# First MLP product of a two-layer transformer trunk by Strassen's 2x2 block form, on one Trainium2 core

## The chip, the cores and the metric

The kernel runs on one core of a Trainium2 chip. The time is the device time of one execution in microseconds (us). Five engines work side by side, each through its own queue of instructions in order: TensorE (PE in the profile, its weight loads PEld), VectorE (DVE), ScalarE (ACT), GpSimd (POOL) and SyncE (SP, which here only issues transfers). Fewer microseconds are better.

## The reference

Two layers work on 512 latent tokens and 256 context tokens of 1024 features. Each has adaLN-modulated RMSNorm, one input projection, a gMLP mixer beside grouped-query attention, an output projection, and then the part that the change touches:

```python
def sqrelu_mlp(h, w1, w2):
    return jnp.square(jax.nn.relu(h @ w1)) @ w2
...
    for l in range(DEPTH):                                   # DEPTH = 2
        last = l == DEPTH - 1
        m_lat = modulation(c, w_mod[l], b_mod[l])
        m_ctx = modulation(c_ctx, w_mod[l], b_mod[l])
        ...
        x_lat = x_lat + ga2 * sqrelu_mlp(modulate(rmsnorm(x_lat, norm2_g[l]), sh2, sc2),
                                         w_ff1[l], w_ff2[l])
        if not last:
            ...
            x_ctx = x_ctx + cga2 * sqrelu_mlp(modulate(rmsnorm(x_ctx, norm2_g[l]), csh2, csc2),
                                              w_ff1[l], w_ff2[l])
    return x_lat
```

`w_ff1[l]` is 1024 x 4096, `w_ff2[l]` 4096 x 1024, all float32. The MLP of layer 0 runs over 768 tokens, that of layer 1 over the 512 latent ones.

## The kernel before

**Products in split form.** Each float32 operand is held as a high part `hi` in TensorE's reduced float32 format and the remainder `lo`. `split` (L207, L208) makes them: ACT casts the raw tile to `hi`, DVE subtracts `hi` from the raw tile for `lo`. A product is three matmuls, hi x hi, hi x lo and lo x hi (`mm`, L203). Activations lie features first: an MLP feature tile is 128 features (partitions) by all tokens, and a product over 1024 input features is 8 x 3 matmuls per token part. Layer 0 has two token parts of 384 columns, layer 1 one of 512.

**Weight stream.** Weights come as blocks of 128x1024 in the order of use (`block_order`). `pump` issues a block's transfer on SP into one of two raw buffers, then splits it into one of four ring slots (`hi` and `lo` tiles). It goes on as long as slots are free; `release` gives a slot back once the last matmul that reads it is written.

**MLP.** Eight chunks of four feature tiles. `ff1` computes one tile with w_ff1 in PSUM tile `pa`, and `relu2` squares its ReLU and splits the square: ACT ReLU (L954) and Square (L959), DVE product (L960) and difference (L961), into a `B` home, of which eight hold two chunks of tiles. `proj4` then takes the four blocks of w_ff2 of the chunk (called first to fourth second-product block below), eight output tiles of 4 x 3 matmuls each per token part, and `gate` (L784) adds each to the residual stream `X` on DVE. In `steady` the first tile of the next chunk is computed before the second product of this chunk, the other three behind it.

**What else runs beside layer 0's MLP.** `mod_wide(1)` computes layer 1's modulation without TensorE: a 256 KB transfer of w_mod rows into one of its raw halves `k` (L354, SP), ACT scales a 128x512 piece by a number per partition (L368, tile `s`), POOL adds it to a sum (L369). `more()` writes the next piece of it at the places where it is called. `consts(1)` (rope tables, norm gains, mixing weights for layer 1) is written before layer 0's steady chunks.

**What sets the order.** The kernel is written through an emission clock (`Flow`), which counts TensorE time and writes put-off work when its turn comes; a scheduler then reorders instructions of an engine, but for engines under `manual_schedule`, which keep the order as written. The first seven chunks of layer 0 are written so for DVE and ACT (`FM0` is 'DA', `FC` 7); the last chunk of layer 0 and all of layer 1 are left to the scheduler. A PSUM or SBUF tile is tracked as a whole: who writes one half of it waits for readers of the other half.

Of the kernel before, what the change touches and what calls it, by code (L numbers as in the profile page):

```python
# [26 lines left out]
# columns of the packed constants  # L27
# [4 lines left out]
# emission lags and periods, in ns of tensor-engine time  # L32
# [9 lines left out]
def once(fn):  # L42
    """fn, but for the first call alone"""
    left = [fn]
    return lambda: left.pop()() if left else None


class Flow:
    """Emission clock: counts tensor-engine time and emits put-off work once its turn has come."""
# [36 lines left out]
    def fill0(self, until):  # L86
        """pass the time without fillers"""
# [4 lines left out]
    def step(self):  # L92
        """one piece of filler"""
# [19 lines left out]
# how pieces of the output projection (o) and of the modulation (m) alternate beside the attention of layer 0  # L113
# [6 lines left out]
def block_order():  # L120
# [3 lines left out]
    for l in range(DEPTH):  # L124
# [36 lines left out]
def trunk(ctx: ExitStack, tc: tile.TileContext, xT, pk1, pk2, rope, wsT, w_mod, w_tok, w_u, w_out, w_ff1, w_ff2, outT):  # L161
# [57 lines left out]
    def convert():  # L219
        """split the oldest block that is held back"""  # L220
# [3 lines left out]
    def pump():  # L224
        while state["live"] < RING and state["pos"] < len(order):
            key = order[state["pos"]]
            if key == ("ctx",):
# [3 lines left out]
                continue  # L231
            src = dram[key[0]]
# [15 lines left out]
            hi = ring.tile([128, 1024], F32R, tag="hi", name=nm("hi"), bufs=RING)  # L248
            lo = ring.tile([128, 1024], F32R, tag="lo", name=nm("lo"), bufs=RING)
# [6 lines left out]
            state["live"] += 1  # L256
# [6 lines left out]
    def take(*key):  # L263
        if not ready:
            settle()
        k, hi, lo = ready.pop(0)
# [7 lines left out]
    def rsqrt(v, n):  # L274
        """1/sqrt of a small positive tile: a bit estimate, a quadratic and a cubic step."""
# [26 lines left out]
    # silu of both conditions  # L302
# [6 lines left out]
    S32 = const.tile([128, 8, 32], F32, name="S32")  # L309
# [266 lines left out]
    def layer(l, h, nxt, K, kv=None, kv0=0):  # L576
# [409 lines left out]
        def ff1(m):  # L986
# [3 lines left out]
            for i, (off, n) in enumerate(dense):  # L990
# [4 lines left out]
                if i == 0:  # L995
                    more()
# [166 lines left out]
```

## Time and profile before

| | |
|---|---|
| median of 3 runs | 1533.48 us (1533.36 to 1533.84) |
| span of the profiled execution | 1530.9 us |
| PE busy, share of the span | 1484.1 us, 97% |
| DVE busy | 957.4 us, 63% |
| ACT busy | 682.6 us, 45% |
| POOL busy | 402.0 us, 26% |

No time of its own is given for the profiled execution; its span is what the profile covers. A row of the costliest groups reads: line, engine, operation, what is written <- what is read, form, count | busy us, mean ns of one | idle us of that engine just ahead of them, with what ended it. A row of the chain reads: start us, length us, engine, tile and line. A row of the timeline reads: start us, length us, engine, line, operation, tiles, form, count. A row of transfers reads: tile <- tensor, queue, count, size of one, median us from issue to landing.

### The profile page before, as it was taken

The numbers are of one execution on the slowest core, as the hardware profiler recorded it, in microseconds if no ns is written. First come the engines' busy times: TensorE is split into PE (matmuls) and PEld (weight loads), VectorE is DVE, ScalarE is ACT, GpSimd is POOL, SyncE is SP. The second block draws the span as 40 slices with busy tenths as digits, with TensorE's granted clock in tenths as the row PEclk, the third lists the DMA queues.
The fourth block names the chain that finished last, engine by engine and source line by source line (L and its number), as shares of the span: only waits on it lengthen the run. The fifth ranks groups of instructions, "written<-read, shape, count | busy, mean of one in ns | idle before, by whom it ended". The sixth has DMA issues, their size and how long they took to land.

```text
span 1530.9 us, 22786 instructions
## 1 busy us (share of the span) xinstructions
PE 1484.1 (97%) x8804; PEld 1321.5 (86%) x8804; DVE 957.4 (63%) x1874; ACT 682.6 (45%) x1142; POOL 402.0 (26%) x362
## 2 busy tenths in 40 slices
PE   6999899999999999999999999998999999999998
PEld 2899686779899999999999998996889888888887
DVE  5868966776855555555555547988796644444443
ACT  3542355564545453545444424535784433322221
POOL 0112320023244545545454603035213000000000
PEclk9999999999999999999999999999999999999999
DMA  9221324321134333333333321221101333332332
GB/s 359 67 74 48 119 91 152 110 83 56 62 108 122 113 123 126 111 118 106 124 109 124 98 68 56 86 80 44 41 1 56 97 96 97 98 97 97 96 98 79
DMA packets 49948, 148.83 MB, mean 97 GB/s; under 512 B 5424, under 2 KB 6832, under 8 KB 49840
## 3 DMA queue, kind: packets, MB, share of 16 engines
q1 hardware_dynamic: 49264, 146.46, 29.9%
q8 instruction: 69, 1.13, 0.3%
q10 hardware_dynamic: 576, 0.92, 0.2%
q14 instruction: 39, 0.32, 0.1%
HBM read 145.26 MB, written 2.10 MB: 96 GB/s over the span
## 4 chain that ended last, share of the span: by engine, by line
PE 82%; DVE 12%; DMA 2%; ACT 2%; issue 1%; POOL 0%; SPq 0%; ACTq 0%; POOLq 0%; DVEq 0%
PE pa L203 51%; PE pb L203 21%; PE pt L844 3%; PE pt L203 3%; PE pb L326 2%; DVE lo L208 1%; DMA X<-in_xT 1%; DMA C<-in_w_mod 1%; DVE X L784 1%; DMA A<-in_w_mod 1%; DVE m L277 1%; PE pt L626 1%; DVE B L961 1%; ACT hi L207 1%; PE pb L865 0%
## 5 line engine op out<-in xcount | busy, mean ns | idle before, releaser
L203 PE MATMUL pa<-A,hi 128*128 128x384 f32 (+2 forms) x1696 | 449.2, 347 | 1.7 <-ACT w L954 0.6
L207 ACT CAST hi<-raw 128x1024 fp32r<-128x1024 f32 x171 | 179.5, 1050 | 409.9 <-PE pa L203 326.3
L208 DVE TENSOR_TENSOR lo<-raw,hi 128x1024 fp32r<-128x1024 f32 x155 | 202.7, 1308 | 215.8 <-ACT hi L207 212.4
L203 PEld LDWEIGHTS pa<-A,hi 128*128 128x128 f32 x1696 | 304.7, 188 | 25.9 <-ACT w L954 1.8
L369 POOL TENSOR_TENSOR C<-C,s 128x512 f32<-128x512 f32 x168 | 240.5, 1463 | 245.0 <-ACT s L368 244.8
L203 PE MATMUL pa<-A,lo 128*128 128x384 f32 (+2 forms) x848 | 293.4, 347 | 1.1 <-DVE lo L208 1.1
L203 PE MATMUL pa<-B,hi 128*128 128x384 f32 (+1 forms) x900 | 246.4, 356 | 4.4 <-DVE X L784 4.4
L203 PEld LDWEIGHTS pa<-B,hi 128*128 128x128 f32 x900 | 162.9, 188 | 21.5 <-DVE X L784 9.2
L784 DVE SCALAR_TENSOR_TENSOR X<-pa,modT,X 128x384 f32<-128x384 f32 (+1 forms) x168 | 88.0, 547 | 143.0 <-PE pa L203 143.0
L203 PEld LDWEIGHTS pa<-A,lo 128*128 128x128 f32 x848 | 159.3, 188 | 12.0 <-DVE lo L208 1.3
L203 PE MATMUL pa<-B,lo 128*128 128x384 f32 (+1 forms) x450 | 158.1, 353 | 0.0
L203 PE MATMUL pb<-B,hi 128*128 128x256 f32 (+2 forms) x600 | 152.3, 340 | 0.4 <-DVE X L784 0.4
L368 ACT ACTIVATE s<-k,silu 128x512 f32<-128x512 f32 x168 | 114.3, 716 | 49.4 <-DMA k<-in_w_mod 27.3
L203 PE MATMUL pb<-hi,A 128*128 128x256 f32 x672 | 126.1, 285 | 0.0
L784 DVE SCALAR_TENSOR_TENSOR X<-pb,modT,X 128x512 f32<-128x512 f32 (+3 forms) x116 | 69.1, 602 | 75.8 <-PE pb L203 75.3
L203 PEld LDWEIGHTS pb<-B,hi 128*128 128x128 f32 x600 | 104.0, 189 | 11.6 <-DVE X L784 1.0
L203 PEld LDWEIGHTS pb<-hi,A 128*128 128x128 f32 x672 | 106.1, 191 | 0.2 <-issue 0.2
L203 PE MATMUL pb<-B,lo 128*128 128x256 f32 (+2 forms) x300 | 101.5, 338 | 0.0
L203 PE MATMUL pb<-lo,A 128*128 128x256 f32 x336 | 95.3, 284 | 0.0
L203 PEld LDWEIGHTS pa<-B,lo 128*128 128x128 f32 x450 | 84.4, 188 | 5.8
L847 DVE TENSOR_TENSOR A<-pt,A 128x384 fp32r<-128x384 f32 (+1 forms) x144 | 73.6, 535 | 16.4 <-ACT A L846 14.4
L846 ACT CAST A<-pt 128x384 fp32r<-128x384 f32 (+1 forms) x144 | 64.6, 469 | 43.3 <-PE pt L844 39.5
(169 smaller groups left out, 2300.3 us busy)
## 6 DMA issues: line engine op xcount, KB each, us to landing
raw<-in_w_ff SPq DMA_DIRECT2D x128, 512.0 KB, 3.5
k<-in_w_mod SPq DMA_DIRECT2D x96, 256.0 KB, 3.0
hi<-in_w_mod SPq DMA_DIRECT2D x32, 512.0 KB, 3.6
raw<-in_w_tok SPq DMA_DIRECT2D x19, 512.0 KB, 3.5
raw<-in_w_out SPq DMA_DIRECT2D x16, 512.0 KB, 3.5
A<-in_w_mod SPq DMA_DIRECT2D x8, 512.0 KB, 9.9
raw<-in_w_u SPq DMA_DIRECT2D x8, 512.0 KB, 3.5
B<-in_w_mod SPq DMA_DIRECT2D x6, 512.0 KB, 10.2
```

Source lines behind the costliest of these rows:

```text
L203: pe.matmul(out, a, b, start=start, stop=stop)
L207: act.copy(hi, src)
L208: (eng or vec).tensor_tensor(out=lo, in0=src, in1=hi.bitcast(F32), op=ALU.subtract)
L277: vec.tensor_scalar(yi, v.bitcast(I32), -0.5, 1595932665.0, op0=ALU.mult, op1=ALU.add)
L326: pe.matmul(ps[q:q + 32, :], S32[:, k, :], w[:, k2 * 512:(k2 + 1) * 512], start=k < ns, stop=k >= KT - ns)
L368: act.activation(p, w, AF.Copy, scale=s)
L369: pool_e.tensor_tensor(out=a, in0=a, in1=p, op=ALU.add)
L626: pe.transpose(p[:, o:o + 128], stk[:, t, hh, c0:c0 + 128].bitcast(F32), ident)
L784: vec.scalar_tensor_tensor(out=xs, in0=src[:, s - off:e - off], scalar=modT[l][:, i * 8 + m, cond:cond + 1], in1=xs, op0=ALU.mult, op1=ALU ...
L844: pe.transpose(tp_[:, (kt - k0) * 128:(kt - k0) * 128 + 128], p[:, kt * 128:kt * 128 + 128], ident)
L846: act.copy(pth[:, k0:k0 + step, d], src)
L847: vec.tensor_tensor(out=ptl[:, k0:k0 + step, d], in0=src, in1=pth[:, k0:k0 + step, d].bitcast(F32), op=ALU.subtract)
```

## The change

Fourteen of the sixteen pairs of MLP feature tiles (m, m + 16) are computed by Strassen's form for 2x2 blocks with seven quadrant products (Winograd's variant, in which sums are shared). The quadrants of the weights are the two halves of the input features by the two tiles of a pair; those of the activations the two halves of the input features by the two halves of the tokens (384 columns each in layer 0, 256 in layer 1). The other two pairs, (0, 16) and (1, 17), are computed as before, as chunk 0, and all chunks now take their tiles in the order 2c, 2c + 16, 2c + 1, 2c + 17 (rows of w_ff2 are laid out to match).

- `pump_pair` loads both weight blocks of a pair, `ra` and `rb`, into the two raw buffers. It splits `ra` as `al` and half of `rb` as `q` (own tiles `qh`, `ql`), and POOL then makes the four sums of weights in place: `rb` becomes the operand `be`, `ra` the operand `ga`. These are split once 9000 ns (`SW`) of emission time have passed and two ring slots are free, or when the pair is taken.
- `ff1_pair` computes the products in this order: A (al, first half), E (q), C (be, first half), B (be, second half), A+ (al, second half, added to A), B+ (ga, first half, added to B), C+ (ga, second half, added to C). A and C are the halves of one PSUM tile `pa`. ACT copies A (L1121) and C (L1125) to SBUF, DVE (and POOL once) adds products to the four output quadrants, and each is squared (`sqrelu`, one DVE operation), cast on ACT (L1089) and split on DVE (L1090); the quadrant of A alone goes through ReLU (L1133) and Square (L1135) on ACT.
- `factors` makes four sums of activations per feature quarter once per layer, during the first chunk: POOL rebuilds float32 activations, DVE subtracts and splits.
- Feature tiles have four homes H0 to H3 for the former eight; the eight B homes hold the sums of activations. Both pairs of a chunk come before its second product, so nothing of the next chunk's first product is computed ahead of it.
- `proj4` with `early` starts its first two output tiles with the first two feature tiles (k = 0, 1), for both, and only then uses the others.
- The constants of layer 1, the attention's mix and copy buffers and the broadcast silu tile move into homes H0 to H3; `consts(1)` moves behind layer 0's last second product. The scratch for dynamic transfers becomes 1024.

```diff
-        o += [("ff1", l, m) for m in range(4)]
+        o += [("ff1", l, m) for m in (0, 16, 1, 17)]
         for ch in range(8):
-            if ch < 7:
-                o.append(("ff1", l, ch * 4 + 4))
+            if ch:
+                o += [("pair", l, 2 * ch + i) for i in range(2)]
             o += [("ff2", l, ch, nb) for nb in range(4)]
-            if ch < 7:
-                o += [("ff1", l, ch * 4 + 4 + i) for i in range(1, 4)]
...
+    def pump_pair(key):
+        _, l, p = key
+        if half["raw"] is None:
+            if state["live"] + 1 > RING or half["busy"]:
+                return False
...
+            ra, rb = raws
+            hi, lo = slot()
+            split(hi, lo, ra)
+            qh, ql = (ring.tile([128, 512], F32R, tag=t, name=nm(t), bufs=1) for t in ("qh", "ql"))
+            split(qh, ql, rb[:, 512:1024])
+            half["busy"] = True
+            a11, a12, a21, a22 = ra[:, 0:512], ra[:, 512:1024], rb[:, 0:512], rb[:, 512:1024]
+            tt = pool_e.tensor_tensor
+            tt(out=a11, in0=a11, in1=a21, op=ALU.subtract)
+            tt(out=a21, in0=a21, in1=a22, op=ALU.add)
+            tt(out=a22, in0=a22, in1=a11, op=ALU.subtract)
+            tt(out=a12, in0=a12, in1=a22, op=ALU.subtract)
+            half["raw"] = (raws, (hi, lo), (qh, ql))
+            half["next"] = fl.vt + PAR["SW"]
+            fl.defer(PAR["SW"], pump)
+        if fl.vt < half["next"] and not half.get("force"):
+            return False
+        if state["live"] + 2 > RING:
+            return False
+        (ra, rb), al, q = half["raw"]
+        be = tuple(slot())
+        split(*be, rb)
+        ga = tuple(slot())
+        split(*ga, ra)
...
+        def ff1_pair(p):
+            (al, q), (be, ga) = take("pair", l, p)
...
+            product(A, al, 0, quad(0, 0), True, True)
+            act.copy(c1_, A)
+            product(E, q, 0, tsum(3), True, True)
+            half["busy"] = False
+            product(C, be, 0, tsum(0), True, True)
+            act.copy(c5, C)
+            more()
+            product(B, be, 512, tsum(1), True, True)
+            release()
+            tt(out=U2, in0=B, in1=c1_, op=ALU.add)
+            product(A, al, 512, quad(1, 0), False, True)
+            release()
+            r = tsm([128, hn])
+            act.activation(r, A, AF.Relu)
+            hd = H[p]
+            act.activation(hd[:, 0, 0:hn], r, AF.Square)
+            tt(out=r, in0=r, in1=r, op=ALU.mult)
+            tt(out=hd[:, 1, 0:hn], in0=r, in1=hd[:, 0, 0:hn].bitcast(F32), op=ALU.subtract)
+            more()
+            product(B, ga, 0, tsum(2), False, True)
+            tt(out=U3, in0=B, in1=c1_, op=ALU.add)
+            t21 = tsm([128, hn])
+            tt(out=t21, in0=E, in1=U3, op=ALU.add)
+            pool_e.tensor_tensor(out=c5, in0=c5, in1=U3, op=ALU.add)
+            put(p + 16, 0, sqrelu(t21))
+            more()
+            product(C, ga, 512, quad(1, 1), False, True)
+            release()
+            tt(out=U2, in0=C, in1=U2, op=ALU.add)
+            put(p, 1, sqrelu(U2))
+            put(p + 16, 1, sqrelu(c5))
+            more()
...
         def steady(chs):
             for ch in chs:
-                if ch < 7:
-                    ff1(ch * 4 + 4)
-                    more()
-                R = [H.pop(ch * 4 + kk) for kk in range(4)]
+                if ch:
+                    ff1_pair(2 * ch)
+                    ff1_pair(2 * ch + 1)
+                R = [H.pop(m) for m in (2 * ch, 2 * ch + 16, 2 * ch + 1, 2 * ch + 17)]
```

**ACT in layer 0.** In the kernel before, two casts of weight blocks (`hi_8337`, of w_ff1, and `hi_8343`, the first block of the second product) stand ahead of the ReLU of a tile, with modulation scalings behind:

```order
L207 CAST hi_8337<-raw_8335 128x1024
L207 CAST hi_8343<-raw_8341 128x1024
L954 ACTIVATE w_8347<-pa_8267 128x768
L959 ACTIVATE B_1434_8268<-w_8347 128x768
L368 ACTIVATE s_8353<-k_4859,silu 128x512
L368 ACTIVATE s_8356<-k_4859,silu 128x512
L368 ACTIVATE s_8386<-k_4859,silu 128x512
L368 ACTIVATE s_8389<-k_4859,silu 128x512
```

In the changed kernel, at the passage from a chunk's first pair to its second: the two casts of the first pair's last quadrants, two scalings, be (`hi_8556`, of the raw tile of rb), ga (`hi_8560`, of that of ra), the first second-product block (`hi_8566`), and then the copies of A and C of the second pair:

```order
L1089 CAST H_1497_8395<-w_8401 128x384
L1089 CAST H_1498_8396<-w_8400 128x384
L420 ACTIVATE s_8550<-k_4914,silu 128x512
L420 ACTIVATE s_8553<-k_4914,silu 128x512
L205 CAST hi_8556<-raw_8441 128x1024
L205 CAST hi_8560<-raw_8439 128x1024
L205 CAST hi_8566<-raw_8564 128x1024
L1121 COPY w_8575<-pa_8572 128x384
L1125 COPY w_8575<-pa_8572 128x384
L420 ACTIVATE s_8616<-k_4914,silu 128x512
L420 ACTIVATE s_8619<-k_4914,silu 128x512
L1133 ACTIVATE s_8647<-pa_8572 128x384
```

The casts of be and ga now stand behind the first pair's tail, the cast of a block that is yet to be loaded stands ahead of the copy of A, and two scalings stand ahead of the ReLU of A.

**PE in layer 0.** Before, the last matmuls of the next chunk's first tile (`pa_8509`) are followed by the second product (`pa_8581`), whose second feature tile is `B_1434`:

```order
L203 MATMUL pa_8509<-A_894_4275,hi_8337 128x384 x2
L203 MATMUL pa_8509<-A_894_4275,lo_8338 128x384
L203 MATMUL pa_8509<-A_895_4276,hi_8337 128x384 x2
L203 MATMUL pa_8509<-A_895_4276,lo_8338 128x384
L203 MATMUL pa_8581<-B_1389_7893,hi_8343 128x384 x2
L203 MATMUL pa_8581<-B_1389_7893,lo_8344 128x384
L203 MATMUL pa_8581<-B_1434_8268,hi_8343 128x384 x2
```

Now, in the second pair of a chunk: the end of E (`pt_8574`), B (`pb_8573`, four feature quarters with be, `hi_8556` and `lo_8557`; the first and the last quarter shown), two matmuls of the second product (`pa_8723`), and C (`pa_8572`, the same PSUM tile as A):

```order
L1101 MATMUL pt_8574<-C_969_4714,ql_8448 128x384
L1101 MATMUL pb_8573<-B_944_4647,hi_8556 128x384 x2
L1101 MATMUL pb_8573<-B_944_4647,lo_8557 128x384
```

```order
L1101 MATMUL pb_8573<-B_968_4713,hi_8556 128x384 x2
L1101 MATMUL pb_8573<-B_968_4713,lo_8557 128x384
L201 MATMUL pa_8723<-H_1497_8395,hi_8566 128x384 x2
L1101 MATMUL pa_8572<-B_944_4647,hi_8556 128x384 x2
L1101 MATMUL pa_8572<-B_944_4647,lo_8557 128x384
```

Two matmuls that read the first second-product block stand in the middle of the pair, ahead of C.

**ACT in layer 1.** Before, casts of weight blocks stand one to five in a row, ahead of the ReLU of tiles that they are not for:

```order
L207 CAST hi_14280<-raw_14278 128x1024
L207 CAST hi_14314<-raw_14312 128x1024
L207 CAST hi_14346<-raw_14344 128x1024
L954 ACTIVATE w_14350<-pa_14318 128x512
L959 ACTIVATE B_2505_14319<-w_14350 128x512
L207 CAST hi_14383<-raw_14381 128x1024
```

Now, from the first pair's ReLU of A (L1133) to the second pair's copy of A (L1121): be and ga of the second pair (`hi_14146`, `hi_14150`) ahead of that ReLU, the first second-product block (`hi_14156`) and the casts of the last quadrants behind it, then the copies; two further block casts ahead of the second pair's ReLU of A:

```order
L205 CAST hi_14146<-raw_14063 128x1024
L205 CAST hi_14150<-raw_14061 128x1024
L1133 ACTIVATE s_14103<-pa_14019 128x256
L1135 ACTIVATE H_2505_14017<-s_14103 128x256
L205 CAST hi_14156<-raw_14154 128x1024
L1089 CAST H_2506_14018<-s_14121 128x256
L1089 CAST H_2505_14017<-w_14023 128x256
L1089 CAST H_2506_14018<-w_14022 128x256
L1121 COPY w_14165<-pa_14162 128x256
L1125 COPY w_14165<-pa_14162 128x256
L205 CAST hi_14268<-raw_14266 128x1024
L205 CAST hi_14274<-raw_14272 128x1024
```

Block casts that wait for a transfer or for a ring slot now stand ahead of ReLUs and copies of the pairs.

More of the change, by code (lines that the diff above doesn't have):

```diff
@@ L255, in pump, with slot @@
             state["pos"] += 1
[L256 removed]
+    def slot():
+        state["live"] += 1
+        return (ring.tile([128, 1024], F32R, tag=t, name=nm(t), bufs=RING) for t in ("hi", "lo"))
+    half = {"raw": None, "next": 0.0, "busy": False}
+    def pump_pair(key):
[3 more added lines that the diff above has]
+                return False
+            raws = []
+            for m in (p, p + 16):
+                raw = ring.tile([128, 1024], F32, tag="raw", name=nm("raw"), bufs=2)
+                nc.sync.dma_start(raw, w_ff1[l, m])
+                raws.append(raw)
+            ra, rb = raws
+            hi, lo = slot()
+            split(hi, lo, ra)
[20 more added lines that the diff above has]
+        split(*ga, ra)
+        half["raw"] = None
+        state["pos"] += 1
+        ready.append((key, (al, q), (be, ga)))
+        return True
     def settle():
@@ L1037, in steady @@
                         more()
-                if not end:
-                    for i in range(1, 4):
-                        ff1(ch * 4 + 4 + i)
-                        more()
+                if end and not last:
+                    K1.append(consts(l + 1))
         ET = mybir.EngineType
```

138 lines of the change are left out of this document (100 added, 38 removed), and 2 rows, old and new, of the table PAR.

## The prediction

> **What bounds the kernel now.** I read the page first, then busy time by stretch, then the chain of work in the two MLPs, then single durations. "First product" is the MLP's product with w_ff1, "second product" the one with w_ff2, "layer 0" and "layer 1" the two layers.
>
> ```profile
> span 1530.9 us, 22786 instructions
> PE 1484.1 (97%) x8804; PEld 1321.5 (86%) x8804; DVE 957.4 (63%) x1874; ACT 682.6 (45%) x1142; POOL 402.0 (26%) x362
> ```
>
> ```profile
> 438.50:849.00 410.50, 406.99 (x2384) 399.85 (x2385) 221.07 (x294) 197.25 (x265) 214.58 (x151) 1.00 0.38 117
> 1222.00:1505.00 283.00, 283.00 (x1251) 234.32 (x1250) 135.62 (x155) 84.22 (x105) 0.00 (x0) 1.00 0.30 95
> ```
>
> The columns of the stretches are length, then busy time of PE, weight loads, DVE, ACT, POOL, then the granted clock (1.00). TensorE is the bound in both MLPs; POOL is half busy in layer 0 and idle in layer 1. The sum is made against the span; 1533.48 - 1530.9 = 2.6 us lie outside it in the median run and are taken over unchanged.
>
> The chain in layer 0, with the start of the second product of three chunks (438.47, 713.76, 851.41):
>
> ```profile
> 438.47 2.36 PE pa L203 x12
> ...
> 648.66 2.08 PE pa L203 x12
> ...
> 707.24 1.06 ACT hi L207
> ...
> 708.33 2.01 DVE lo L208
> 710.34 0.88 DVE w L960
> ...
> 711.24 1.94 DVE B L961
> 713.18 0.54 DVE X L784
> ...
> 713.76 2.35 PE pa L203 x12
> ...
> 851.41 2.34 PE pa L203 x12
> ```
>
> From 438.47 to 851.41 are six chunks, 68.82 us each. Twelve 384-column matmuls take 2.08, so 0.1733 each, and a chunk has 384 of them: 66.56. The other 2.26 us per chunk is this run: a weight split, the squared ReLU of a first-product tile and a residual update stand one behind the other on DVE, and TensorE waits. Layer 1 has no such gap:
>
> ```profile
> 1265.54 32.64 PE pa L203 x144
> ...
> 1309.06 32.64 PE pa L203 x144
> ```
>
> ```profile
> 1176.14 0.40 PE L203 MATMUL pa<-A,hi 128*128 128x256 f32 x2
> ...
> 1176.50 0.40 PE L203 MATMUL pa<-A,hi 128*128 128x256 f32 x2
> ```
>
> A 512-column matmul takes 32.64 / 144 = 0.2267, a chunk 43.52 = 192 x 0.2267. Three 256-column matmuls take 1176.50 - 1176.14 = 0.36, so 0.120 each.
>
> **Matmuls removed.** Layer 0: 7 products of 12 for 8, at 0.1733, so 12 x 0.1733 = 2.08 a pair, 29.1 for 14. Layer 1: 48 x 0.2267 = 10.88 becomes 84 x 0.120 = 10.08, 0.80 a pair, 11.2 for 14. Sum 40.3. The 2.26 us runs (7 x 2.26 = 15.8) go too: no first-product tile is left whose ReLU stands right before the second product. With all else hidden: 1533.5 - 40.3 - 15.8 = 1477. Bare chunks would be 360 x 0.1733 = 62.4 and 168 x 0.120 + 96 x 0.2267 = 41.9.
>
> **What takes its place.** The new orders decide this. Durations:
>
> ```profile
> L207 ACT CAST hi<-raw 128x1024 fp32r<-128x1024 f32 x171 | 179.5, 1050 | 409.9 <-PE pa L203 326.3 <-PE pb L203 53.0 <-PE pt L203 15.4
> L368 ACT ACTIVATE s<-k,silu 128x512 f32<-128x512 f32 x168 | 114.3, 716 | 49.4 <-DMA k<-in_w_mod 27.3 <-POOL C L369 21.8
> L846 ACT CAST A<-pt 128x384 fp32r<-128x384 f32 x128 | 58.6, 481 | 35.7 <-PE pt L844 31.9 <-PE pb L203 2.3
> L959 ACT ACTIVATE B<-w 128x256 fp32r<-128x256 f32 x12 | 5.0, 414 | 0.3
> ```
>
> ```profile
> L847 DVE TENSOR_TENSOR A<-pt,A 128x384 fp32r<-128x384 f32 x128 | 67.0, 549 | 12.7 <-ACT A L846 10.7
> L784 DVE SCALAR_TENSOR_TENSOR X<-pa,modT,X 128x384 f32<-128x384 f32 x42 | 25.7, 612 | 13.9 <-PE pa L203 13.9
> L784 DVE SCALAR_TENSOR_TENSOR X<-pa,modT,X 128x256 f32<-128x256 f32 x42 | 19.9, 475 | 0.0
> L961 DVE TENSOR_TENSOR B<-w,B 128x256 fp32r<-128x256 f32 x12 | 4.8, 417 | 0.1
> ```
>
> ```profile
> 1309.96 1.23 DVE L208 TENSOR_TENSOR lo<-raw,hi 128x1024 fp32r<-128x1024 f32 x1
> ```
>
> ```profile
> raw<-in_w_ff SPq DMA_DIRECT2D x128, 512.0 KB, 3.5
> k<-in_w_mod SPq DMA_DIRECT2D x96, 256.0 KB, 3.0
> ```
>
> *Layer 0, second pair of a chunk*, t = 0 when TensorE ends the first pair. ACT and DVE hold the order as written, so the splits of be and ga stand behind the first pair's tail. DVE adds to 0.6 (0.55) and squares to 1.2 (0.61), ACT casts to 1.7 (0.48), DVE subtracts to 2.25, squares the next quadrant to 2.85, ACT casts to 3.35, then scales two modulation rows (2 x 0.72; none, two or four by chunk): 4.8. The cast of be ends at 5.8, of ga at 6.9; DVE's remainders 1.23 later, 7.1 and 8.3. The first second-product block lands in the buffer that ga was made in: transfer 8.3 to 11.8, cast to 12.85. ACT's copy of product A stands behind this cast: 13.35. TensorE: A and E end at 4.16; B waits for be, 7.1 to 9.2; the next two matmuls need the block cast at 12.85; C waits for the copy, 13.35 to 15.4; four matmuls of B+, then A+ to 18.2. C+ waits for the ReLU of A, which stands on ACT behind two scalings whose rows are queued on SP behind the third second-product block; its buffer comes free when DVE has split the first block (14.1), so 14.1 + 3.0 + 1.4 + 0.5 = 19.0, hidden by the rest of B+ (19.6). C+ ends at 21.7. Seven products and the two matmuls are 14.9, so 6.8 us are waited.
>
> *Then the second product.* 16 matmuls are ready: 24.5. ACT squares, casts, scales and splits until the second block's cast ends at 25.3 and the third's at 26.2, 1.0 us of wait with what runs between. The pair's last remainders are due by 31.4, when TensorE has used up the rest (32.1). Together 7.8. DVE also meets POOL here:
>
> ```profile
> 641.72 8.37 POOL L369 TENSOR_TENSOR C<-C,s 128x512 f32<-128x512 f32 x6 [1.67 <-ACT s L368]
> 685.27 5.86 POOL L369 TENSOR_TENSOR C<-C,s 128x512 f32<-128x512 f32 x4 [9.59 <-ACT s L368]
> ```
>
> ```profile
> 642.04 1.93 DVE L961 TENSOR_TENSOR B<-w,B 128x768 fp32r<-128x768 f32 x1
> ...
> 693.86 0.96 DVE L961 TENSOR_TENSOR B<-w,B 128x768 fp32r<-128x768 f32 x1
> ```
>
> The same subtraction takes 0.96 with POOL idle and 1.93 beside it. One such meeting per chunk adds 1 us: 8.8, for the six chunks in written order 52.8. From below: without scalings ahead and without meetings some 6; from above, with four scalings and three meetings, 12.
>
> [...]
>
> *Layer 0, last chunk*: freely scheduled, its splits stand before the tail; between 0 and 8, I take 4, as in layer 1.
>
> *Layer 1*, t = 0 at the first pair. The second pair's be needs the ring slot that al leaves at five products (7.2): cast 8.25, ga 9.3, ga's remainder 10.7, transfer to 14.2, cast 15.2, three casts of 0.41 to 16.45, copy of A 16.9. The first pair's C+ (due 8.64) waits for a ReLU behind the two casts, 9.7 to 11.15; the second pair's A, E and half of B end at 14.75, C waits to 16.9. A+ ends at 20.5 and frees the next slot; two casts and a ReLU later C+ starts at 22.95 and ends at 24.4, against a bare 20.16: 4.2. DVE then has two splits, the tail and a split (seven additions and subtractions of 0.42, four products of 0.48): last remainders at 29.7 and 30.1, TensorE ready for them at 28.6: 1.1. Sum 5.3 a chunk, 37.1 for seven. From below: 2 (only the wait of C); from above 7. What was there before:
>
> ```profile
> ACT hi L207 <- PE pa L203: 171.6, 46, 4.4
> ```
>
> ACT waited for TensorE to free a ring slot, the splits ran one to four blocks ahead; in the new pairs three blocks are tied to two buffers for raw weights.
>
> *Sums of inputs* (16 subtractions and splits on DVE, eight 768-column additions on POOL) run beside 21.8 us of 512-column matmuls in the first chunk: 0 to 6, I take 2, since the next pair needs them only after a whole second product. *Constants of layer 1* move behind layer 0's last matmul, where DVE is already what TensorE waits for:
>
> ```profile
> 911.04 19.38 PE pb L203 x95
> ...
> 936.76 1.10 PE pt L454 x2
> ```
>
> TensorE waits from 930.4 to 936.8 there. A transfer (3.5) and eleven small DVE operations join that queue; other projections cover most: 0 to 8, I take 4. The 4 homes, the shared mix buffer and the smaller scratch cost nothing by themselves: the homes' cost is the tail priced above, and TensorE, reading in order, reaches a home again only after a whole second product.
>
> **Sum.** 1533.5 - 40.3 - 15.8 + 52.8 + 4 + 37.1 + 2 + 4 = 1577.
>
> **Rivals.**
>
> *Blocks in time (faster).* If the first second-product block were in place when C is due, the chain at 8.3 to 13.35 would go; layer 0 keeps about 2 us a chunk (the wait for be), layer 1 about 1. 1477 + 14 + 7 + 6 = 1504. For it: all transfers of the kernel before are early. Against: the raw buffer is free only after ga's split. It decides once waits fall below 56 us in all, 4 a chunk, half of what I find. 0.14.
>
> *Layer 1 hidden.* Layer 0 as priced, layer 1 at its lower end of 2: 1577 - 23 = 1554. 0.13.
>
> *POOL.* [...] 0.10.
>
> ```profile
> L743 POOL TENSOR_TENSOR C<-s,C 128x512 f32<-128x512 f32 x10 | 12.8, 1287 | 26.0 <-DVE s L739 19.6 <-DVE m L285 6.1 <-DVE mv L716 0.4
> L369 POOL TENSOR_TENSOR C<-C,s 128x512 f32<-128x512 f32 x168 | 240.5, 1463 | 245.0 <-ACT s L368 244.8
> ```
>
> *Waits equal savings*: within 0.2% (3 us, about what a measurement of this kernel can tell from no change): 0.04.
>
> **Numbers.** Forecast 0.59, its own range 1560 to 1595. Slower: 0.59 + 0.13 + 0.10 = 0.82; faster 0.14; same 0.04. The range runs from 1512, in the middle of the faster case, to 1606: it leaves out some 0.08 below and 0.07 above.
>
> **What would show it.** Right: chunks near 71 us in layer 0 and near 47 in layer 1; on the chain of waits, casts of raw weights released by a transfer (ACT hi waiting for DMA raw) ahead of a copy from pa; TensorE idle released by ACT copies and by DVE splits, four-fold in each second pair; PE's share near 92%. Wrong: chunks at 62 to 64 and 42 to 43, and casts still released by TensorE. The weakest terms are how much of layer 1's 5.3 is real and how long ACT's scalings wait for POOL.

## The result, and the profile after

| | before | after |
|---|---|---|
| median | 1533.42 us (1532.38 to 1533.84, 4 runs) | 1663.43 us (1661.88 to 1664.91, 4 runs) |
| span of the profiled execution | 1530.9 us | 1663.1 us |

The ratio is 1.0846, 95% interval 1.083 to 1.0861: 130 us slower, where 44 us were forecast.

The page of the changed kernel, its span, its busy times and the granted clock in 40 slices (10 tenths are full speed, shown as 9):

```profile
span 1663.1 us, 24243 instructions
PE 1499.0 (90%) x9140; PEld 1331.5 (80%) x9140; DVE 1140.4 (69%) x2218; ACT 741.6 (45%) x1314; POOL 627.6 (38%) x518
PEclk9999999999798979898989999999999799999999
```

TensorE is busy 15 us longer although 29.1 + 11.2 us of matmuls are gone. Its granted clock (the share of full speed that it is allowed to run at) dips in slices of both MLPs, where the rows of before had 1.00.

Where the 132 us of span arose can be had from three marks in each trace: the first ReLU of layer 0's MLP (394.2 before, 395.3 after), the first matmul of its last second product (904.7, 1008.1) and the first ReLU of layer 1's MLP (1180.1, 1285.9). Layer 0's MLP took 510.5 and takes 612.7, +102.2. The stretch between the MLPs went from 275.4 to 277.8, +2.4. Layer 1's MLP, to its last matmul (1526.6, 1658.8), went from 346.5 to 373.0, +26.5.

Layer 0's chunks: ACT's ReLU of A in the first pair of chunk 1 and of chunk 7, and the busy times between them (six chunks; the columns are length, then PE, weight loads, DVE, ACT, POOL, then the granted clock, the share of the DMA engines and GB/s):

```profile
493.13 0.49 ACT L1133 ACTIVATE s<-pa 128x384 f32<-128x384 f32 x1 [3.74 <-PE pa L1101]
...
988.43 0.48 ACT L1133 ACTIVATE s<-pa 128x384 f32<-128x384 f32 x1
```

```profile
493.10:988.40 495.30, 423.70 (x2260) 396.84 (x2255) 302.85 (x416) 221.70 (x332) 305.87 (x213) 0.92 0.31 97
```

That is 82.55 us a chunk for 68.82 before. POOL is busy 51 us of each, for 36 before (214.58 in six chunks), and the granted clock is 0.92. TensorE is busy for 70.6 us of each chunk and idle for 11.9.

Layer 1's chunks in the chain, first and last of seven starts of the same run of matmuls:

```profile
1335.23 5.44 PE pa L201 x24
...
1601.25 5.44 PE pa L201 x24
```

266.02 / 6 = 44.34 a chunk for 43.52 before. So these six chunks hold only 4.9 of layer 1's 26.5 us. Most of the rest, and a part of layer 0's, is in chunk 0, where TensorE stands for a ReLU in each layer (timeline of TensorE):

```profile
438.96 1.22 PE L201 MATMUL pa<-A,hi 128*128 128x512 f32 x2 [14.59 <-ACT w L1029]
```

```profile
1318.23 0.80 PE L201 MATMUL pa<-A,hi 128*128 128x256 f32 x2 [15.79 <-ACT w L1029]
```

At one passage from a first to a second pair in layer 0, the timelines of ACT, POOL, DVE, SP's queue and TensorE show much of the chain that the forecast described, with POOL all through it:

```profile
745.57 4.82 POOL L421 TENSOR_TENSOR C<-C,s 128x512 f32<-128x512 f32 x3
...
750.42 0.72 ACT L420 ACTIVATE s<-k,silu 128x512 f32<-128x512 f32 x1 [0.83 <-POOL C L421]
...
752.05 1.62 DVE L1093 SCALAR_TENSOR_TENSOR w<-w 128x384 f32<-128x384 f32 x1
...
755.36 1.98 ACT L205 CAST hi<-raw 128x1024 fp32r<-128x1024 f32 x2
756.42 3.38 DVE L206 TENSOR_TENSOR lo<-raw,hi 128x1024 fp32r<-128x1024 f32 x2 [1.21 <-ACT hi L205]
756.44 1.01 PE L1101 MATMUL pb<-B,hi 128*128 128x384 f32 x2 [6.35 <-ACT hi L205]
758.73 6.26 SPq L246 DMA_DIRECT2D raw<-in_w_ff  x3
762.33 1.05 ACT L205 CAST hi<-raw 128x1024 fp32r<-128x1024 f32 x1 [4.99 <-PE pb L1101]
763.42 0.62 PE L201 MATMUL pa<-H,hi 128*128 128x384 f32 x2 [1.14 <-ACT hi L205]
```

Scalings on ACT wait for POOL ahead of the casts of be and ga (755.36), TensorE stands 6.35 us for be, then the first second-product block is loaded (issued at 758.73) and cast at 762.33, and only then do the two matmuls that stand ahead of C start.

The cast of be starts 9.6 us after TensorE's last matmul of the first pair (745.76), where the forecast had 4.8. Most of these 4.8 us can be read from DVE, which has few pauses in the first pair's tail and whose operations take longer there while POOL is busy. The same two operations in the first and in the second pair of this chunk, the second time with POOL idle:

```profile
743.01 1.44 DVE L1136 TENSOR_TENSOR s<-s 128x384 f32<-128x384 f32 x1 [2.27 <-ACT H L1135]
744.49 1.53 DVE L1137 TENSOR_TENSOR H<-s,H 128x384 fp32r<-128x384 f32 x1
...
770.37 0.56 DVE L1136 TENSOR_TENSOR s<-s 128x384 f32<-128x384 f32 x1 [5.28 <-ACT H L1135]
770.97 0.56 DVE L1137 TENSOR_TENSOR H<-s,H 128x384 fp32r<-128x384 f32 x1
```

With the square of 1.62 shown above and two smaller cases, DVE loses 3.7 us so between 743.01 and 753.67.

### The profile page after: what moved, and what is told of

Read it like the earlier page. It is cut to its first block, busy times and chain, and to the rows that moved or that the text cites. A ratio compares the mean times of both kernels' runs of the same rounds, so it can differ in the third digit from the quotient of the medians.

```text
span 1663.1 us, 24243 instructions
## 1 busy us (share of the span) xinstructions
PE 1499.0 (90%) x9140; PEld 1331.5 (80%) x9140; DVE 1140.4 (69%) x2218; ACT 741.6 (45%) x1314; POOL 627.6 (38%) x518
## 4 chain that ended last, share of the span: by engine, by line
PE 48%; DVE 23%; ACT 9%; POOL 8%; DMA 6%; issue 5%; SPq 0%; ACTq 0%; POOLq 0%; DVEq 0%
PE pa L201 18%; PE pb L201 17%; DVE lo L206 5%; PE pa L1101 4%; ACT hi L205 4%; DMA raw<-in_w_ff 4%; POOL C L421 2%; PE pt L915 2%; ACT s L420 2%; PE pb L378 2%; PE pb L1101 1%; POOL raw L288 1%; PE pt L201 1%; POOL raw L287 1%; DVE s L1081 1%
## 5 line engine op out<-in xcount | busy, mean ns | idle before, releaser
L201 PE MATMUL pa<-H,hi 128*128 128x384 f32 (+2 forms) x1056 | 298.9, 363 | 22.7 <-DVE X L837 9.8
L201 PEld LDWEIGHTS pa<-H,hi 128*128 128x128 f32 x1056 | 192.9, 191 | 53.0 <-ACT hi L205 10.3
L201 PE MATMUL pa<-H,lo 128*128 128x384 f32 (+2 forms) x528 | 186.7, 356 | 0.0
L837 DVE SCALAR_TENSOR_TENSOR X<-pa,modT,X 128x384 f32<-128x384 f32 (+2 forms) x174 | 91.2, 549 | 100.9 <-PE pa L201 100.9
L1101 PE MATMUL pa<-A,hi 128*128 128x384 f32 (+1 forms) x672 | 150.4, 313 | 9.2 <-ACT s L1133 8.3
L1101 PEld LDWEIGHTS pa<-A,hi 128*128 128x128 f32 x672 | 112.7, 190 | 14.3 <-ACT s L1133 10.5
L1101 PE MATMUL pb<-B,hi 128*128 128x384 f32 (+1 forms) x392 | 97.1, 336 | 29.6 <-ACT hi L205 29.5
L201 PE MATMUL pb<-H,hi 128*128 128x512 f32 (+2 forms) x368 | 108.5, 373 | 6.5 <-ACT hi L205 6.0
L201 PEld LDWEIGHTS pa<-H,lo 128*128 128x128 f32 x528 | 100.1, 190 | 7.1
L1101 PE MATMUL pa<-A,lo 128*128 128x384 f32 (+1 forms) x336 | 103.7, 309 | 0.0
L201 PEld LDWEIGHTS pa<-A,hi 128*128 128x128 f32 x352 | 61.1, 196 | 40.4 <-ACT w L1029 34.0
```

What stands on the lines that cost most here:

```text
L201: pe.matmul(out, a, b, start=start, stop=stop)
L837: vec.scalar_tensor_tensor(out=xs, in0=src[:, s - off:e - off], scalar=modT[l][:, i * 8 + m, cond:cond + 1], in1=xs, op0=ALU.mult, op1=ALU ...
L1101: pe.matmul(dst, a, b, start=first and k == 0 and i == 0, stop=last_ and k == 3 and i == 2, skip_group_check=True)
```

## The experiments

Each run's time is compared with the changed kernel's 1663.43; the kernel before, run beside every group of them, had medians of 1532.38 to 1533.60. "Chunk" is the span between the marks shown above, over six. Line numbers shift by a few with the edits.

### The sums of activations in chunk 0

Where they are written:

```diff
                 if pi:
-                    factors()
...
+                    if ch == 0 and n in fat:        # fat: 0, 2, 4, 6 in layer 0, 0 to 3 in layer 1
+                        factors([fat.index(n)])
```

> Edit: the sums of activations (16 per layer, with their splits) are no longer written ahead of the first chunk's second token part but in four pieces behind the first output tiles of chunk 0's second product. Theory S, the sums hold the buffers and the DVE queue in front of chunk 0's ReLUs, so TensorE stands for 14.6 us in layer 0 and 15.8 us in layer 1 and then runs at half clock for a while: both stalls go, about 24 us in layer 0 and 19 us in layer 1, 1620 us. Rival S', the same DVE and POOL work only moves the stall into chunk 0's second product or the first pair: 1650 to 1660 us.

Measured: 1666.22. The rival held (a little above its range). Layer 1's MLP gained 7 us, layer 0's lost 9. TensorE no longer stands for the ReLU but for residual updates that DVE does later, and then in the first pair for the sums themselves:

```profile
465.65 1.01 PE L201 MATMUL pa<-H,hi 128*128 128x384 f32 x2 [7.29 <-DVE X L837]
477.66 1.28 PE L1100 MATMUL pt<-C,qh 128*128 128x384 f32 x2 [5.27 <-ACT C L205]
```

Which buffers the ReLUs use:

```diff
...
+                    own = [x[:, i] for x in (unit("C1", [128, 2, 512], F32), tk([128, 2, 512], F32)) for i in range(2)]
                     factors()
...
-                        relu2(ms[m], dst[m], off, n)
+                        relu2(ms[m], dst[m], off, n, own[m][:, 0:n] if pi else None)
```

> Edit: the four ReLUs of chunk 0's second token part write to buffers of their own (a free home and a free raw buffer) in place of the three buffers that the sums of activations also use. Theory B, TensorE's stalls of 14.6 and 15.8 us in front of these ReLUs are a wait for a buffer: they fall below 3 us each and the half-clock stretch behind them goes, 1620 to 1630 us. Rival D, the DVE work of the sums has to be done before the first pair in any case: the first pair or the first second product waits instead, 1645 to 1663 us.

Measured: 1662.51. The rival held: in layer 0 the 14.59 us became waits of 4.24, 4.02 and some shorter ones at the same place, and one of 2.94 behind them. The ReLUs stand in queues behind the sums, whatever buffer they write.

How much of the work is done:

```diff
             for k in range(4):
+                if k:
+                    TT.append(TT[0])
+                    continue
                 hv = []
```

> Edit: of the sums of activations only the first quarter of the features is made, and its tiles stand in for the other three (the products are then not those of the reference); all matmuls stay. Theory S2, the DVE and POOL work of the sums itself costs the stalls of chunk 0 in both layers wherever it is written: three quarters of some 24 us in layer 0 and 17 us in layer 1 go, 1630 to 1635 us. Rival, chunk 0 is slow for the modulation and the raw buffers: 1655 us or more.

Measured: 1627.88, 35.6 us less, as theory S2 has it. From the first ReLU of the MLP to the first pair's ReLU of A, layer 0 went from 97.8 to 80.8 and layer 1 from 71.7 to 54.2, 17 us each; the chunks stayed (82.4 and 44.2). If the last quarter costs as much, the sums cost some 46 us in all, an estimate. The 17 us include what TensorE loses at half clock in and behind its stalls (clock 0.50 from 428.4 to 448.9 and from 1305.6 to 1326.1 in the changed kernel).

### The order and the raw buffers in layer 0's pairs

```diff
             put(p + 16, 0, sqrelu(t21))
+            half["force"] = True
+            settle()
+            half["force"] = False
             more()
             product(C, ga, 512, quad(1, 1), False, True)
```

> Edit: the splits of be and ga for the next pair are written between a pair's B+ and C+, ahead of the rest of its tail, in place of behind it. Theory O, the written order makes them late: the wait for be in the second pair (about 5 us and a half-clock stretch behind it) goes, a layer-0 chunk falls from 81.5 to about 72, 1600 us. Rival P, POOL and the modulation work make the sums of weights late in any order: chunks stay at 78 or more, 1640 to 1660 us.

Measured: 1644.33, chunk 78.9. The rival held as to time and chunk, and theory O as to the wait: TensorE's wait for be went from 29.5 us in six chunks to 2.9, but the wait of the second product for the first block's cast rose to 31.8, from 7.5 (waits of TensorE over six chunks, first in the changed kernel, then with the early splits):

```profile
PE pb L1101 <- ACT hi L205: 29.5, 6, 6.4
```

```profile
PE pa L201 <- ACT hi L205: 31.8, 6, 6.2
...
PE pb L1101 <- ACT hi L205: 2.9, 1, 2.9
```

Of the 22 us that these six chunks gained, 13 are not waiting: TensorE needs 410.35 us for the same matmuls, in place of 423.70, at a granted clock of 0.95.

```profile
493.00:966.20 473.20, 410.35 (x2260) 390.08 (x2254) 310.85 (x416) 219.80 (x333) 310.86 (x213) 0.95 0.32 102
```

Then the block's cast was put behind the copies of A and C (a flag that holds the stream back between them):

```diff
+            if state["live"] >= RING or half.get("hold"):
...
+            half["hold"] = True
             product(A, al, 0, quad(0, 0), True, True)
             act.copy(c1_, A)
...
             act.copy(c5, C)
+            half["hold"] = False
+            fl.defer(0.0, pump)
```

> Edit: besides the early splits of the earlier run (1644 us), the cast of the first second-product block is written behind the second pair's copies of A and C in place of ahead of them. Theory K, product C stands for the block's transfer and cast through the copy of A: 2 to 3 us a chunk in layer 0, 1622 to 1632 us. Rival, the block is due a few us later in any case: 1638 to 1646 us.

Measured: 1643.93. The rival held as to time, and not for its reason: TensorE now stands for the copy of A, which is itself behind the first pair's casts and scalings.

```profile
PE pa L1101 <- ACT w L1122: 29.4, 7, 5.6
```

Three kernels with three different operations at the head of the wait, at 29 to 32 us over six chunks each: the wait does not belong to one instruction in ACT's queue. What stands behind it, POOL beside DVE and the raw buffers, is the matter of the next runs.

### POOL and the modulation of layer 1

All of it out but the first scaling of each sum:

```diff
                         if k == 0:
                             act.activation(a, w, AF.Copy, scale=s)
-                        else:
-                            p = tsm([128, 512])
-                            act.activation(p, w, AF.Copy, scale=s)
-                            pool_e.tensor_tensor(out=a, in0=a, in1=p, op=ALU.add)
+                        elif k > KT:
+                            pass
```

> Edit: of layer 1's modulation only the first scaling of each sum is left; the other 168 scalings on ACT and 168 additions on POOL are left out, so the modulation is not computed. The transfers stay. Theory P: with POOL free for the sums of weights and no scaling ahead of the casts, a layer-0 chunk falls from 81.5 to about 72, 1600 us. Theory O: casts still stand behind the tail and the block transfer, chunks fall only by the two to four scalings ahead of be (1.5 to 3 us each) to 77 or 78, about 1635 us.

Measured: 1607.71, chunk 73.4. Theory P. Then POOL's additions alone (only the last of these removed lines out):

> Edit: of layer 1's modulation only POOL's 168 additions are left out (it is not computed); the scalings on ACT and the transfers stay. Theory Q, POOL alone is the cause (its additions and ACT's waits for them): as without the whole modulation, 1600 to 1612 us. Rival, the scalings on ACT that stand ahead of the casts are the cause: 1635 to 1660 us.

Measured: 1616.44, chunk 74.8, 4 us above theory Q's range and far from the rival: 47 of those 56 us go with POOL's additions. Busy times of six chunks (as above) and DVE's remainders of weight blocks, with the additions (first of the two groups) and without:

```profile
490.50:939.40 448.90, 409.58 (x2260) 391.84 (x2252) 252.80 (x416) 218.72 (x333) 79.31 (x61) 0.95 0.33 107
```

```profile
L206 DVE TENSOR_TENSOR lo<-raw,hi 128x1024 fp32r<-128x1024 f32 x61 | 102.4, 1702 | 65.7 <-ACT hi L205 65.6
```

```profile
L206 DVE TENSOR_TENSOR lo<-raw,hi 128x1024 fp32r<-128x1024 f32 x61 | 73.1, 1223 | 66.4 <-ACT hi L205 66.4
```

The same 416 DVE instructions take 302.85 us beside POOL and 252.80 without: 8.3 us a chunk, of which 0.48 on each of ten splits. The 36 residual updates of 128x384, which read one operand from PSUM, keep their length (with the additions, then without):

```profile
L837 DVE SCALAR_TENSOR_TENSOR X<-pa,modT,X 128x384 f32<-128x384 f32 x36 | 21.9, 609 | 2.6 <-PE pa L201 2.6
```

```profile
L836 DVE SCALAR_TENSOR_TENSOR X<-pa,modT,X 128x384 f32<-128x384 f32 x36 | 22.0, 611 | 2.9 <-PE pa L201 2.9
```

How the 47 us divide between longer DVE operations, ACT's waits for POOL and sums of weights that stand in POOL's queue was not measured apart. The scalings out and the additions in:

```diff
-                            p = tsm([128, 512])
-                            act.activation(p, w, AF.Copy, scale=s)
-                            pool_e.tensor_tensor(out=a, in0=a, in1=p, op=ALU.add)
+                            pool_e.tensor_tensor(out=a, in0=a, in1=w, op=ALU.add)
```

> Edit: the 168 scalings on ACT are left out and POOL adds the unscaled rows (the modulation is not that of the reference); POOL's work stays whole. Theory L, POOL's additions lengthen DVE's operations beside them (a 128x1024 remainder takes 1.70 us in layer 0's pairs, 1.22 without the additions): the time stays at 1640 to 1663 us. Theory A, ACT's waits for POOL (51 us over six chunks) with casts queued behind them are what costs: 1605 to 1625 us.

Measured: 1679.57, chunk 85.5, beyond both ranges and on theory L's side. Nothing holds POOL's additions back now, and they stand ahead of the sums of weights: ACT's casts wait for those for 40.6 us, longest 12.3 (24.9 with no modulation at all), and for transfers (behind the late splits) for 80.4 (28.8 in the changed kernel).

```profile
ACT hi L205 <- DMA raw<-in_w_ff: 80.4, 14, 12.8
...
ACT hi L205 <- POOL raw L289: 40.6, 5, 12.3
```

So taking away ACT's 51 us of waiting for POOL saves nothing while POOL's work stays. Whether these waits have a cost of their own is not shown, since POOL's queue runs in another order here. The work on DVE instead of POOL, first the modulation, then the sums of weights:

```diff
-"MP": [0, 1]
+"MP": []
```

> Edit: layer 1's modulation is scaled and summed by one DVE operation a piece (168 of them, 128x512) in place of a scaling on ACT and an addition on POOL. Theory Q, the modulation hurts by POOL's time and ACT's waits for POOL: a layer-0 chunk falls from 81.5 to 74 or 75, about 1615 us. Rival, DVE is as short as POOL was: 24 operations of 0.7 us a chunk (17 us) stand ahead of splits and subtractions, 1650 to 1690 us.

```diff
-            tt = pool_e.tensor_tensor
+            tt = vec.tensor_tensor
```

> Edit: the four sums of weights of each pair are made on DVE in place of POOL, in both layers. Theory W, these sums are late since they stand between modulation additions in POOL's queue: the wait for be shrinks by about 4 us a chunk in layer 0, 1630 us. Rival, the order of the casts sets the wait, and DVE's 5 us more a chunk delay the tail: 1660 to 1680 us.

Measured: 1698.37 (chunk 87.6) and 1698.25 (chunk 88.7; layer 1's fell from 44.4 to 43.2). Both lie above both ranges, on the rivals' side: in layer 0 DVE has no room either. The kernel before without the additions:

> The kernel before with POOL's 168 modulation additions left out (the modulation is not computed). Theory: POOL's work costs the kernel before next to nothing, since its splits run blocks ahead; at most a part of the 2.26 us a chunk goes: 1518 to 1533 us. Rival, POOL costs both kernels alike: about 1485 us.

Measured: 1526.37 against 1532.74, ratio 0.9958 (0.9942 to 0.9973), as the theory has it. DVE's remainders there shrank too, by 0.24 us each,

```profile
L208 DVE TENSOR_TENSOR lo<-raw,hi 128x1024 fp32r<-128x1024 f32 x49 | 71.7, 1464 | 93.8 <-ACT hi L207 93.8
```

```profile
L208 DVE TENSOR_TENSOR lo<-raw,hi 128x1024 fp32r<-128x1024 f32 x49 | 59.8, 1221 | 110.4 <-ACT hi L207 110.4
```

and TensorE hid most of it. The same additions cost 6 us where splits run ahead and 47 where they are on the chain.

### The clock

```diff
             product(E, q, 0, tsum(3), True, True)
+            if p % 2 and not last:
+                product(E, q, 0, tsum(3), True, True)
+                product(E, q, 0, tsum(3), True, True)
```

> Edit: in the second pair of each chunk of layer 0 product E is computed three times over into the same place (24 more matmuls a pair, 168 in all, 29 us of TensorE work), which fills the start of the wait for be. Theory C, the half-clock stretches are brought on by TensorE's idle time: with the wait filled they go in the second pairs, and the time falls to about 1640 us though 29 us of work is added. Rival, the stretches do not depend on idle time or the waits are shorter than the filling: 1663 to 1690 us.

Measured: 1664.43 (two runs, 1659.06 and 1669.81, so a change of under some 5 us can't be seen). Half of theory C held. Through layer 0's MLP the stretches at half clock shrank from 99 to 58 us in the clock records (a mean clock of 0.92 and 0.95; over the whole execution 0.959 and 0.971), so some of them go when idle time is filled. In the changed kernel the one behind the wait of 6.35 us reads (first the length, then the busy times, then the clock):

```profile
752.80:762.90 10.10, 4.58 (x12) 3.56 (x12) 5.22 (x4) 4.21 (x6) 4.60 (x4) 0.50 0.39 130
```

But the time did not fall. With the wait filled, B starts 2.34 us after its predecessor, still at the cast of be, and the next wait grows from 1.14 to 2.16:

```profile
752.38 1.01 PE L1101 MATMUL pb<-B,hi 128*128 128x384 f32 x2 [2.34 <-ACT hi L205]
...
760.39 0.62 PE L201 MATMUL pa<-H,hi 128*128 128x384 f32 x2 [2.16 <-ACT hi L205]
```

In this passage the matmuls at half clock were run in time that the block's transfer and cast take anyway. In the changed kernel's layer 0 the clock went to half in each of the seven gaps of 4.2 us or more (4.24 to 14.59). It also went to half, for 3.4 us each, in or right behind gaps of 2.20 us (695.2 to 697.4), 1.90 (798.3 to 800.2) and 2.11 (975.9 to 978.1), and once more from 858.5 to 861.9, with no gap over 0.66 in the 10 us before. Three 384-column matmuls of a product took 0.96 us at half clock (759.21 to 760.17) and 0.52 at full (743.68 to 744.20). By these two layer 0's 99 us would be up to 45, an estimate; what a matmul loses there is a cost only where TensorE, not its suppliers, is the last to end.

### What is left

Three edits together, no modulation, a quarter of the sums and the early splits:

> Edit: three earlier edits at once: no modulation of layer 1 but its first scalings, one quarter of the sums of activations, early splits. If the three causes are separate, their gains of 56, 36 and 19 us add: 1553 us. If they are one wait seen three times: 1585 to 1600 us. Either way above the 1526 us of the kernel before without POOL's additions unless the pairs have more slack than the waits show.

Measured: 1544.00, chunk 69.3, below both ranges. The gains add, and a little more: 119.4 us for 110.4 singly. A third raw buffer for the MLP's blocks (every third block goes to a home that is free without the modulation):

```diff
+    def third():
+        turn3[0] += 1
+        if turn3[0] % 3 == 0:
+            return unit("C1", [128, 1024], F32)
+        return ring.tile([128, 1024], F32, tag="raw", name=nm("raw"), bufs=2)
```

> Edit: as the run without the modulation (1608 us), but with a third buffer for raw MLP blocks in a home that this leaves free, and without the modulation's transfers behind the first of each sum. Theory R, the first second-product block cannot be loaded before ga is split: with a third buffer its cast waits for no transfer, a layer-0 chunk falls from 73.3 to about 68 and a layer-1 chunk from 44.4 to about 43, 1565 to 1575 us. Rival, the order of the casts on ACT sets the wait: 1595 to 1608 us.

Measured: 1574.33, chunks 69.5 and 43.2. Theory R: 33 us, with no instruction moved by hand, 22.9 of them in layer 0's MLP (553.3 to 530.4) and 8.5 in layer 1's. The modulation's transfers are out as well here; of layer 1, where there are none in either kernel, the 1.2 us a chunk are the buffer's alone. For layer 0 the trace of the run without the modulation speaks for the buffer too: from 560 to 860 us each MLP block's transfer was issued within 0.1 us of the end of a DVE remainder, which frees a raw buffer. And the casts' wait for transfers, in that run

```profile
ACT hi L205 <- DMA raw<-in_w_ff: 27.0, 13, 4.7
```

over six chunks, is not among the waits with the third buffer.

> Edit: the three edits of the run before the last and the third raw buffer. Theory: with POOL, sums, order and buffers out of the way the chunks come near their bare 62.4 and 41.9 us: 1500 to 1520 us, so the form of the products saves what the forecast said and the rest is feeding it. Rival, waits of ACT and DVE in the pairs stay at 5 us a chunk or more: 1540 to 1555 us.

Measured: 1536.70 (8 runs), chunks 68.9 and 43.15. Neither range. The third buffer gives 7.3 us here, and next to none of it in layer 0, whose MLP goes from 511.2 to 510.2 us (layer 1's from 355.2 to 346.2). With the early splits the casts of layer 0 waited for transfers for only 6.0 us in six chunks, so there was little left for the buffer to gain: the two remove the same wait, and their gains do not add. TensorE's chunk of layer 0 has 65.8 us of busy time, and what it waits for is the cast of second-product blocks (13.4 us over six chunks):

```profile
475.20:888.30 413.10, 394.51 (x2258) 381.81 (x2252) 251.81 (x416) 122.85 (x180) 78.72 (x61) 0.98 0.20 68
```

```profile
PE pa L201 <- ACT hi L205: 13.4, 6, 3.2
```

With all of this out of the way the changed form is still 10 us behind the 1526.4 of the old form without the additions. No kernel that leaves nothing out was faster than the one before. What holds the last 6 us a chunk (68.9 against 62.4 bare) was not taken apart further; TensorE is idle for 3.1 of it (18.6 of the 413.1 us above).

## Why the prediction was wrong, by its steps

**Matmuls removed: right.** Start-to-start spacings add to 63.1 us a chunk in layer 0 (with the modulation's small matmuls) for 67.3 before, and to 41.9 for 43.5 in layer 1: 4.2 and 1.6, as in the sum.

**Sums of inputs, "0 to 6, I take 2": failed.** Three quarters of them cost 35.6. The step counted what TensorE had to do meanwhile (21.8 us of matmuls), and not that ACT and DVE have chunk 0's ReLUs, squares, splits and residual updates to do in the same time. In layer 0 DVE was at the sums from 415.3 to 443.7, and a subtraction beside POOL took 2.18 us in place of 0.55 (timeline of DVE, first and last of the 16):

```profile
415.30 2.18 DVE L1081 TENSOR_TENSOR s<-w 128x384 f32<-128x384 f32 x1 [1.75 <-POOL w L1071]
...
443.14 0.55 DVE L1081 TENSOR_TENSOR s<-w,s 128x384 f32<-128x384 f32 x1
```

**"One such meeting per chunk adds 1 us": mis-sized several times over.** Without POOL's additions a chunk is 7.7 us shorter. The rows with 1.93 and 0.96 were read rightly, and then one meeting was counted, though POOL was to be busy half of the time or more and each subtraction and square of DVE on a chain could meet it; in the passage shown above such meetings cost 3.7 us ahead of be alone. Not all of the 7.7 need be meetings. The rival "POOL" rested on the author's estimate of what a split loses where it meets POOL, and no run shows that term; what the runs showed is 0.48 us more on the mean for a remainder of 128x1024, and a kernel 47 us faster without the additions.

**Second pair of layer 0: the mechanism right but for one buffer.** The late splits of be, the block's transfer behind a split and the copy behind the block's cast stand in the trace in the order forecast. The block does not land in ga's buffer but in be's: its transfer is issued at 758.73, when be's remainder has ended (758.66) and ga's has not (759.80), and so in each second pair between 560 and 860 us. The step had it 1.2 us too late there. Written earlier the splits move to the next wait (19 us for the early splits, nothing for the copy). That the raw buffers tie them was the point: a third one gave 33 us without the modulation, though none in layer 0 once the splits were early and the sums cut. Without POOL's part and the scalings the chunk is 73.4 for a forecast of 71.2.

**The granted clock, 1.00 in the rows of before, was carried over unsaid.** It fell to 0.92. Of a layer-0 chunk TensorE is idle for 11.9 us, where the sum has 8.8 of waits, and busy for 70.6, where the sum has 62.4. So more of the miss in a chunk shows as matmuls that take longer than as waiting. How much of that would be saved at full clock stays open: filling the waits cut the half-clock time and saved nothing, while with the early splits 13 us of shorter matmuls came with a gain of 22.

**Layer 1's pairs, "5.3 a chunk": too dear.** 44.34 less 41.9 is 2.4, the lower end of 2 nearly, so the rival "Layer 1 hidden" was right on the pairs. **Constants, 4:** the stretch between the MLPs grew by 2.4.

**The old waits, "The 2.26 us runs (7 x 2.26 = 15.8) go too": failed, in size and in kind.** 2.26 is a chunk's length less its 384 matmuls, but TensorE waited for only 4.4 of these 13.6 us in six chunks. And the waits for residual updates did not go; they grew to 9.8 (first the kernel before, then the changed one, over six chunks):

```profile
PE pa L203 <- DVE X L784: 4.4, 5, 1.2
```

```profile
PE pa L201 <- DVE X L837: 9.8, 10, 1.9
```

In terms of the sum: layer 0's chunks at 82.55 in place of 71.2 are 68 us, the sums some 44 more than priced, layer 1's pairs 20 less, the constants 2 less. That is 90 us for the 86 that were missed; the extrapolated quarter of the sums and the last chunk of layer 0 are not known better than that. The 68 us hold POOL's part, the waits that did not go and the lower clock together.

## What to carry to other kernels

A form with fewer products is paid for in operand preparation, and the price is not only its count but also whether the prepared operands have a buffer to wait in: ask for each new operand how many blocks it can run ahead, before counting matmuls. Where an engine's operations are seen to take longer beside another at work (here DVE's remainder of 128x1024, 1.70 us with POOL's additions and 1.22 without), price the meeting at every operation on the new chain and for as long as the other engine is busy, not once. Work that costs little beside an engine with slack can cost many times that once the slack is used up; POOL's additions cost the kernel before 6 us and the new one 47.

## What the runs showed of the hardware

TensorE's granted clock fell to 0.50 for 10 us within 3 us of the start of an idle stretch of 6.35 us, and stayed there for 6.5 us after TensorE went on. Three idle stretches of 1.90 to 2.20 us also had half clock in or right behind them, for 3.4 us, and one such fall had no gap over 0.66 us in the 10 us before it. Three 384-column matmuls took 0.96 us at half clock, 0.52 at full. Filling idle time with repeated matmuls cut the time at half clock by 41 us and the kernel's time by nothing that its two runs could show. DVE's subtraction of two SBUF tiles of 128x1024 took 1.22 us on the mean without POOL's additions (POOL 18% busy in six chunks of layer 0) and 1.70 with them (POOL 62% busy); a residual update of 128x384 that reads PSUM took 0.61 in both cases.
